# A two-layer gated encoder on one core: ACT, VectorE and GpSimd ordered by a list scheduler inside the kernel, and a feed-forward input projection with 512 weight columns moving

## The chip, the cores and the metric

One core of a Trainium2 chip runs one program. The metric is the device time of one execution in microseconds; where several executions are given, their median counts.

## What is computed

The reference is a bidirectional encoder trunk of two layers on 256 tokens of width 1024, all in float32. In the reference's words, cut to what matters (`B` is 1, `S` 256, `D` 1024, the hidden width `FFN_HIDDEN` 2816):

```python
for l in range(DEPTH):                       # 2 layers
    h = rms_norm(x, norm_mix_pre[l])
    (c_q, c_kv, k_rope, sc_b, sc_c, sc_x, cf_a, cf_g, gm_u, gm_v, gate_logits) = split(h @ w_in[l])
    y_a = mla_branch(c_q, c_kv, k_rope, ...) @ w_o_mla[l]       # 8-head attention
    y_b = short_conv_branch(sc_b, sc_c, sc_x, ...) @ w_o_sc[l]  # 3 taps
    y_c = conformer_branch(cf_a, cf_g, ...) @ w_o_cf[l]         # 31 taps, layer norm, silu
    y_d = gmlp_branch(gelu(gm_u), gelu(gm_v), ...) @ w_o_gm[l]  # spatial gating
    g = sigmoid(gate_logits + gate_b[l])
    merged = g[0] * y_a + g[1] * y_b + g[2] * y_c + g[3] * y_d
    x = x + rms_norm(merged @ w_out[l], norm_mix_post[l])
    f_g, f_u = split(rms_norm(x, norm_ffn_pre[l]) @ w_ffn_in[l])
    x = x + rms_norm((silu(f_g) * f_u) @ w_ffn_out[l], norm_ffn_post[l])
```

## The kernel before, in words

**Numbers.** TensorE reads its operands in a reduced format (fp32r), so every weight and every activation is split into a high part (a cast on ACT) and a low part (raw minus high, on VectorE), and each product is three matmuls: high by high, high by low, low by high (lines 207 to 209 in `group`; 458 to 460 and 880 to 882 are the same three written out). Attention's two products (lines 677 and 703), the spatial gating (570) and all transposes against an identity (214) are plain float32.

**Weights.** They arrive in units of about 1 MB, 2048 columns of 128 partitions (`unit_list`, class `Weights`). A unit is loaded into one of 4 raw buffers by a DMA of the SP queue (line 138), cast to `hi` on ACT (line 173, in two pieces of 1024) and subtracted to `lo` on VectorE (line 176), into one of 5 pairs of buffers; `use` hands a pair out, `free` gives it back and starts the next. The SP queue is in order: a load that waits for a raw buffer holds those behind it, the rows of gains and biases (`brow`, `gain`) too.

**TensorE.** There are two ways of a projection. In `b_unit` the weights stand still (128 columns) and all 256 tokens move: one matmul writes 128x256, and the result comes out transposed, with the features on the partitions. In the other a tile of 128 tokens (`hth`, `htl`) stands still and 512 weight columns move: one matmul writes 128x512, and what a later product needs transposed goes through TensorE's transposes. The feed-forward input uses the second way for the first 512 hidden units (line 850 on) and `b_unit` for the other 2304: nine blocks of 256 units, each a gate and an up matrix (lines 853 to 858 follow them: silu, product, split).

**Order.** TensorE's and SP's instructions run in the order of the program. Side work on TensorE (attention, the conformer's transposes, the spatial gating, the turns of a tile) is written as generators; `start` puts one in a heap with a due time, and `tick` after each group of three matmuls resumes those that are due by a clock of counted matmul times, with fixed waits (STEP 9, ROPE 14, GMS 12, PACE 2 and so on). The four AV matmuls of a head pair (`values`, line 703) are yielded singly. ACT, VectorE and GpSimd are put in order by the tile framework, by program order; the conformer's 120 tap operations per layer (line 526, VectorE) are held back by a priority of 100, and are issued two at a time. PSUM has 4 banks `pb` for projections and 4 `psd` for side work.

**Places that the steps touch.** `gt` (line 789) adds the gate's bias and frees a bank; `cn` (408) is the normed query and key compression and frees two; `xn` (539) is the conformer's normed row and is what the transposes after it read.

Of the kernel before, what the change touches and what calls it, by code (L numbers as in the profile page):

```python
# [44 lines left out]
def unit_list():  # L45
# [34 lines left out]
    for j in range(2, FH // 256):  # L80
        for o in (0, FH):
            add("w_ffn_in", 0, D, slice(o + 256 * j, o + 256 * (j + 1)))
# [12 lines left out]
def hybrid_encoder(ctx: ExitStack, tc: tile.TileContext, wts, x_in, pos, invf, cols, rows, wst, out):  # L95
    nc = tc.nc
    act, dve, pool, pe = nc.scalar, nc.vector, nc.gpsimd, nc.tensor
# [6 lines left out]
    LAG = 1.0  # L104
    LATE, PACE = 100, 2.0
    WARM = 34
    P1 = 3.0
    TRS = 7.0
    GMS = 12.0
    STEP = 9.0  # L110
    APART = 1.5
    ROPE = 14.0
    NORM = 8.0
    MTURN = 2.5
# [16 lines left out]
    def bank(s="pb"):  # L131
        return ps.tile([P, 512], F32, tag="pb", name=nm(s), bufs=4)

    def sbank(s="psd"):
        return ps.tile([P, 512], F32, tag="psd", name=nm(s), bufs=4)

    def load(dst, src):
        tc.keep_in_program_order(nc.sync.dma_start(dst, src))
# [8 lines left out]
    class Weights:  # L147
        def __init__(self):
            self.nd = self.ns = self.n = self.nf = 0
            self.splits = {}  # L150
            self.raw, self.parts = {}, {}

        def load(self, i):
            l, u = divmod(i, NU)
            w = widths[u]
# [4 lines left out]
            for c in range(0, w, step):  # L160
                load(t[:, c : c + step], src[:, c : c + step])
            self.raw[i] = t

        def split(self, i):
# [13 lines left out]
        def fill(self, apart=0.0):  # L178
            while self.ns < min(self.nf + B_HI, L * NU):
                while self.nd < min(self.ns + B_RAW, L * NU):  # L180
                    self.load(self.nd)
                    self.nd += 1
                self.splits[self.ns] = start(self.split(self.ns), apart * self.ns)
                self.ns += 1

        def use(self, n):
            i = self.n
            self.n += 1
            drain(self.splits.pop(i))
            w = widths[i % NU]  # L190
            return tuple(a[:, :w].rearrange("p (k n) -> p k n", n=n) for a in self.parts.pop(i))
# [7 lines left out]
    def split(hi, lo, src):  # L199
        act.copy(hi, src)  # L200
        dve.tensor_tensor(lo, src, hi, op=ALU.subtract)  # L201

    def group(o, terms, first=True, last=True):
        n = len(terms)
        cost = 3 * o.shape[-1] / 2370.0 if len(o.shape) == 2 else 3 * S / 2370.0
        for i, (lh, ll, rh, rl) in enumerate(terms):
# [3 lines left out]
            tick(cost)  # L210

    def transposes(o, ins, rows_out=P):
        for j, a in enumerate(ins):
            pe.transpose(out=o[:rows_out, j * P : (j + 1) * P], in_=a, identity=ident)  # L214
            clock[0] += 0.11
# [7 lines left out]
    def rstd_of(r, ms, eps=EPS):  # L223
        pool.tensor_scalar(r, ms, eps, None, op0=ALU.add)
        pool.tensor_tensor(r, r, mhalf[:, : ms.shape[-1]], op=ALU.pow)
# [37 lines left out]

    def rope_tables():
        pi = small(T, "pi")
        pii = sb.tile([P, T], I32, tag="pii", name="pii")
        for t in range(T):
            load(pii[:, t : t + 1], pos[0, t * P : (t + 1) * P].rearrange("(p o) -> p o", o=1))
        dve.tensor_copy(pi, pii)
        fr = small(16, "fr")  # L270
        load(fr, invf)
# [23 lines left out]
    def pre_norm(t, g):  # L295
# [3 lines left out]
        act.activation(h, x[:, t, :], AF.Square, scale=D ** -0.5, accum_out=ss)  # L299
        rstd_of(r, ss)  # L300
        for j in range(2):
            c = slice(512 * j, 512 * (j + 1))
            dve.scalar_tensor_tensor(h[:, c], x[:, t, c], r, g[:, c], op0=ALU.mult, op1=ALU.mult)

        def turn():
            for j in range(2):
                b = sbank()
                transposes(b, [h[:, 512 * j + P * k : 512 * j + P * (k + 1)] for k in range(4)])
                bv = b.rearrange("p (k n) -> p k n", n=P)
                split(hth[:, t, 4 * j : 4 * j + 4, :], htl[:, t, 4 * j : 4 * j + 4, :], bv)  # L310
            yield None
# [3 lines left out]
    def post_norm(t, banks, g, store=False):  # L315
# [4 lines left out]
        for j in range(2):  # L320
            c = slice(512 * j, 512 * (j + 1))
            sq = slot(s="sq")
            act.activation(sq, banks[j], AF.Square, scale=D ** -0.5, accum_out=ss[:, j : j + 1])
            if j == 0:
                pool.tensor_scalar(s1, ss[:, 0:1], EPS, None, op0=ALU.add)
            dve.tensor_tensor(y[:, c], banks[j], g[:, c], op=ALU.mult)
        rstd_of(r, ss[:, 1:2], s1)
        for j in range(2):
            c = slice(512 * j, 512 * (j + 1))
            dve.scalar_tensor_tensor(x[:, t, c], y[:, c], r, x[:, t, c], op0=ALU.mult, op1=ALU.add)  # L330
            if store:
                nc.sync.dma_start(out[t * P : (t + 1) * P, c], x[:, t, c])
# [16 lines left out]
    @contextmanager  # L349
    def later(n):  # L350
        at = tc.cur_priority
        tc.cur_priority = at + n
        yield
        tc.cur_priority = at

    clock = [0.0]
    waiting = []

    def start(g, after=0.0):
        heapq.heappush(waiting, (clock[0] + after, nm("g"), g))  # L360
        return g

    def tick(us):
        clock[0] += us
        while waiting and waiting[0][0] <= clock[0]:
            due, _, g = heapq.heappop(waiting)
            after = next(g, None)
            if after is not None:
                heapq.heappush(waiting, (max(due + after, clock[0] + min(after, 0.3)), nm("g"), g))

    def drain(g):
        for i, w in enumerate(waiting):
            if w[2] is g:
                waiting.pop(i)
# [596 lines left out]
```

## Time and profile before

| | |
|---|---|
| median of 3 runs | 972.03 us (971.9 to 972.37) |
| the profiled execution, its own time | 973.39 us |
| its span, first to last instruction | 971.6 us |
| TensorE (PE) busy | 955.2 us, 98% of the span |
| weight loads of TensorE (PEld) | 860.4 us, 89% |
| VectorE (DVE) | 672.5 us, 69% |
| ACT | 477.2 us, 49% |
| GpSimd (POOL) | 46.1 us, 5% |
| read from HBM | 177.63 MB, 184 GB/s over the span |

Matmuls are pipelined and their ends are modelled, so the busy time of PE overlaps itself: what a matmul costs is read from the start of one to the start of the next. A wait in brackets behind a row is idle time of the engine before it, with what ended it. A float32 matmul leaves two records (two passes), a transpose and a matmul of split parts one. DVE is VectorE.

### The profile page before, as it was taken

What the parts mean: (1) busy time and instruction counts of PE and PEld (TensorE: products, weight loads), DVE (VectorE), ACT (ScalarE), POOL (GpSimd) and SP (SyncE); (2) the same over time, 40 slices, a digit from 0 to 9 for tenths busy, and PEclk for the clock granted to TensorE, in tenths of its full rate; (3) what the DMA queues carried; (4) which work ended last, traced back from release to release, by engine and by line L of the source; (5) the groups of instructions that cost most, each with busy time, mean ns of one, the idle gap of its engine ahead of it and who ended that gap; (6) DMA issues with size and microseconds to landing.
All of it is one profiled execution on the core that took longest, in us unless ns stands there. A gap on an engine that the chain in (4) does not pass through costs nothing.

```text
span 971.6 us, 14463 instructions
## 1 busy us (share of the span) xinstructions
PE 955.2 (98%) x5890; PEld 860.4 (89%) x5890; DVE 672.5 (69%) x998; ACT 477.2 (49%) x712; POOL 46.1 (5%) x87
## 2 busy tenths in 40 slices
PE   8999999999999999999999999999999999999997
PEld 7999987888888999998889999888888889999885
DVE  5789999676757655554377899986767675555432
ACT  6555654564445644443365655545544554444421
POOL 1100000010002000000110000000000110000000
PEclk9999999999999999999999999999999999999999
DMA  8765455435654655564268554554365366555601
GB/s 345 274 239 196 152 183 175 162 130 217 206 184 174 217 174 180 193 234 167 100 228 292 174 174 162 173 178 159 141 237 185 122 213 233 191 174 174 224 15 44
DMA packets 29731, 179.62 MB, mean 185 GB/s; under 512 B 3680, under 2 KB 3808, under 8 KB 10208
## 3 DMA queue, kind: packets, MB, share of 16 engines
q1 hardware_dynamic: 29664, 178.69, 52.3%
q8 instruction: 46, 0.75, 0.3%
q14 instruction: 21, 0.17, 0.1%
HBM read 177.63 MB, written 1.05 MB: 184 GB/s over the span
## 4 chain that ended last, share of the span: by engine, by line
PE 86%; DVE 10%; DMA 1%; issue 1%; POOL 1%; ACT 0%; SPq 0%; DVEq 0%; POOLq 0%
PE pb L207 22%; PE pb L209 22%; PE pb L208 22%; PE acc L881 4%; PE acc L880 4%; PE acc L882 4%; DVE yc L526 4%; DVE lo L176 4%; PE psd L214 2%; PE psd L677 1%; PE pb L460 1%; PE pb L459 1%; PE pb L458 1%; PE av L703 1%; DMA brow<-in_rows_dram 1%
## 5 line engine op out<-in xcount | busy, mean ns | idle before, releaser
L176 DVE TENSOR_TENSOR lo<-raw,hi 128x1024 fp32r<-128x1024 f32 (+4 forms) x321 | 379.0, 1200 | 143.2 <-ACT hi L173 143.2
L173 ACT CAST hi<-raw 128x1024 fp32r<-128x1024 f32 (+4 forms) x321 | 323.6, 1035 | 304.5 <-issue 191.1
L207 PE MATMUL pb<-hth,hi 128*128 128x256 f32 x960 | 274.3, 286 | 0.0
L209 PE MATMUL pb<-hth,lo 128*128 128x256 f32 x960 | 271.7, 283 | 0.0
L208 PE MATMUL pb<-htl,hi 128*128 128x256 f32 x960 | 271.6, 283 | 0.0
L208 PEld LDWEIGHTS pb<-htl,hi 128*128 128x128 f32 x960 | 184.0, 192 | 0.3
L207 PEld LDWEIGHTS pb<-hth,hi 128*128 128x128 f32 x960 | 184.0, 192 | 0.3
L209 PEld LDWEIGHTS pb<-hth,lo 128*128 128x128 f32 x960 | 183.9, 192 | 0.0
L207 PE MATMUL pb<-hi,hth 128*128 128x512 f32 x352 | 143.8, 409 | 2.4 <-DVE gt L789 2.4
L209 PE MATMUL pb<-hi,htl 128*128 128x512 f32 x352 | 137.5, 391 | 0.0
L208 PE MATMUL pb<-lo,hth 128*128 128x512 f32 x352 | 137.3, 390 | 0.0
L526 DVE SCALAR_TENSOR_TENSOR yc<-zc,hcol,yc 128x241 f32<-128x241 f32 (+14 forms) x240 | 97.7, 465 | 0.0
L209 PEld LDWEIGHTS pb<-hi,htl 128*128 128x128 f32 x352 | 66.1, 188 | 14.5 <-DVE htl L201 0.3
L207 PEld LDWEIGHTS pb<-hi,hth 128*128 128x128 f32 x352 | 66.3, 188 | 13.9 <-DVE gt L789 2.7
L208 PEld LDWEIGHTS pb<-lo,hth 128*128 128x128 f32 x352 | 66.4, 189 | 11.5
L880 PE MATMUL acc<-hi,fh 128*128 128x512 f32 x176 | 68.6, 390 | 0.0
L881 PE MATMUL acc<-lo,fh 128*128 128x512 f32 x176 | 68.5, 389 | 0.0
L882 PE MATMUL acc<-hi,fl 128*128 128x512 f32 x176 | 68.5, 389 | 0.0
L880 PEld LDWEIGHTS acc<-hi,fh 128*128 128x128 f32 x176 | 33.0, 188 | 6.8
L881 PEld LDWEIGHTS acc<-lo,fh 128*128 128x128 f32 x176 | 33.1, 188 | 6.8
L882 PEld LDWEIGHTS acc<-hi,fl 128*128 128x128 f32 x176 | 33.0, 188 | 6.8
L858 DVE TENSOR_TENSOR f<-f,pb 128x512 f32<-128x512 f32 x18 | 12.4, 687 | 37.7 <-PE pb L209 37.7
(185 smaller groups left out, 1107.0 us busy)
## 6 DMA issues: line engine op xcount, KB each, us to landing
raw<-in_wts_dram SPq DMA_DIRECT2D x152, 1024.0 KB, 4.8
brow<-in_rows_dram SPq DMA_DIRECT2D x24, 256.0 KB, 5.0
gain<-in_rows_dram SPq DMA_DIRECT2D x8, 512.0 KB, 5.7
raw<-in_wts_dram SPq DMA_DIRECT2D x3, 816.0 KB, 4.2
raw<-in_wts_dram SPq DMA_DIRECT2D x2, 768.0 KB, 7.6
raw<-in_wts_dram SPq DMA_DIRECT2D x2, 544.0 KB, 6.2
x<-in_x_dram SPq DMA_DIRECT2D x2, 512.0 KB, 6.0
out_dram<-x SPq DMA_DIRECT2D x4, 256.0 KB, 2.0
```

Source lines behind the costliest of these rows:

```text
L173: act.copy(h[:, c:e], raw[:, c:e])
L176: dve.tensor_tensor(lo[:, c:e], raw[:, c:e], h[:, c:e], op=ALU.subtract)
L207: pe.matmul(o, lh, rh, start=(first and i == 0), stop=False)
L208: pe.matmul(o, lh, rl, start=False, stop=False)
L209: pe.matmul(o, ll, rh, start=False, stop=(last and i == n - 1))
L214: pe.transpose(out=o[:rows_out, j * P : (j + 1) * P], in_=a, identity=ident)
L458: pe.matmul(o, lh, wh[:, k % 3, c], start=(k == 0), stop=False)
L526: dve.scalar_tensor_tensor(y[:, f, a:e], ft2(zc[j])[:, f, a + k - CPAD : e + k - CPAD], cw[:, ff, k : k + 1], y[:, f, a:e], op0=ALU.mult, ...
L858: dve.tensor_tensor(f, f, b, op=ALU.mult)
L880: pe.matmul(o, lh, w[0][:, k, c], start=st, stop=False)
L881: pe.matmul(o, lh, w[1][:, k, c], start=False, stop=False)
L882: pe.matmul(o, ll, w[0][:, k, c], start=False, stop=sp)
```

## The change

**The scheduler.** Calls on ACT, VectorE, GpSimd and on SP's stores no longer emit instructions. They go into a list with a modelled cost and a rank. `Tensor.step` advances a clock by a modelled time for each matmul and then lets `pump` issue, engine by engine, the operation that can start first by the model, and the one of lowest rank among those ready within 0.01 us. Ranks: -0.5 for the norms, 0 for the split of a weight unit that is next to be used, 1 for the rest, 2 for the conformer's taps, 3 for splits further ahead. The order so found is the program's: all five engines then run in order. Loads are issued when the split that frees their buffer is issued in the model. In SP's queue the first row of gains of the second layer (`brow`, read by `cn`) so stands behind six weight loads of that layer, before behind eight; on ACT the order holds nine table loads in place of eight.

**TensorE's side work.** A generator now yields what it needs (`need`), and `poll` resumes it when the model says that this is written and a bank is free; the fixed waits are gone except STEP (9 to 7). `values` yields after two AV matmuls with nothing to wait for, so all four of a head pair follow each other.

**The feed-forward input.** All hidden units are done with tokens standing and 512 weight columns moving (the last block has 256 gate and 256 up columns); each result is transposed on TensorE and split from PSUM (`f_turn`).

The core of the diff:

```diff
+    def cost_act(op, outs, ins):
+        return width(outs[0]) / 1200.0 + 0.195 + 0.05 * (len(ins) > 1) + 0.19 * (len(outs) > 1)
+    def cost_dve(op, outs, ins):
...
+        return n / 960.0 + 0.16 + 0.05 * (op == "scalar_tensor_tensor")
+    def cost_pool(op, outs, ins):
+        return 0.57 if op == "tensor_tensor" else 0.28
...
+    def issue(o):
...
+        at[e] = t = max(at[e], o.ready()) + o.cost
+        for r in o.outs:
+            mark(done, r, t + 0.08)
...
+        o.emit()
+    def event(until):
...
+            t = min(f[0] for f in free)
+            if t <= until and (best is None or t < best[0]):
+                best = t, min((o for f, o in free if f <= t + 0.01), key=Op.order)
...
+        issue(best[1])
...
+    class Tensor:
+        def step(self, out, ins, us):
+            regs, to = [region(v) for v in ins], region(out)
+            flush(clashes([to], regs))
+            t = max([clock[0], opened.get(out.name, 0.0)] + [when(done, r) for r in regs])
+            clock[0] = t + us
...
+            pump(clock[0])
...
+            def rank():
+                return 0 if i <= self.n + NEAR else 3
             for c, e in spans:
-                act.copy(h[:, c:e], raw[:, c:e])
-            for c, e in spans:
-                yield LAG
-                dve.tensor_tensor(lo[:, c:e], raw[:, c:e], h[:, c:e], op=ALU.subtract)
+                act.copy(h[:, c:e], raw[:, c:e], rank=rank)
+                dve.tensor_tensor(lo[:, c:e], raw[:, c:e], h[:, c:e], op=ALU.subtract, rank=rank, then=self.more if e == w else None)
...
-                        with later(LATE):
-                            dve.scalar_tensor_tensor(y[:, f, a:e], ...)
-                        n += 1
-                        if n % 2 == 0:
-                            yield PACE
+                        dve.scalar_tensor_tensor(y[:, f, a:e], ..., rank=2)
...
             for t in range(T):
-                yield 2.0
+                yield need(*yc)
...
                 for j in range(2):
                     h = 2 * hp + j
                     for kc in range(T):
                         i = 2 * j + kc
                         pe.matmul(av[:, DN * h : DN * (h + 1)], ...)
-                        clock[0] += 0.06
-                        yield 0.3
+                    yield need()
...
-        for j in range(2, FH // 256):
-            b = b_unit()
+        for j in range(1, FH // 512):
+            bs = [bank() for _ in range(T)]
+            both(bs)
+            f = [slot(s="f") for _ in range(T)]
+            for t in range(T):
+                act.activation(f[t], bs[t], AF.Silu)
+            bs = [bank() for _ in range(T)]
+            both(bs)
+            hs, ls = hidden(2)
+            for t in range(T):
+                dve.tensor_tensor(f[t], f[t], bs[t], op=ALU.mult)
+                fts.append(start(f_turn(t, f[t], hs, ls)))
```

**VectorE, first gate of the first layer's short-convolution branch.** Before (`gt` are the two gates, `yc` the conformer's taps, `lo` the splits of weights, `m` the merged sum):

```order
L789 TENSOR_TENSOR gt_1667<-pb_1568,brow_1566 128x512
L176 TENSOR_TENSOR lo_1678<-raw_1459,hi_1677 128x1024 x2
L526 SCALAR_TENSOR_TENSOR yc_507<-zc_505,hcol,yc_507 128x250
L526 SCALAR_TENSOR_TENSOR yc_506<-zc_504,hcol,yc_506 128x249 x2
L526 SCALAR_TENSOR_TENSOR yc_507<-zc_505,hcol,yc_507 128x249 x2
L526 SCALAR_TENSOR_TENSOR yc_506<-zc_504,hcol,yc_506 128x248 x2
L176 TENSOR_TENSOR lo_1723<-raw_1544,hi_1722 128x1024 x2
L789 TENSOR_TENSOR gt_1670<-pb_1569,brow_1566 128x512
```

Now (`o` is an attention output, `rs` its sums):

```order
L175 TENSOR_TENSOR lo_1461<-raw_1394,hi_1460 128x1024 x2
L175 RECIPROCAL rs_1699<-sums_1293 128x8
L175 TENSOR_TENSOR gt_1703<-pb_1591,brow_1589 128x512
L175 TENSOR_TENSOR o_1700<-av_1469,rs_1699 128x512
L175 TENSOR_TENSOR gt_1704<-pb_1592,brow_1589 128x512
L175 SCALAR_TENSOR_TENSOR m_1577<-gt_1703,pb_1705 128x512
L175 SCALAR_TENSOR_TENSOR yc_481<-zc_479,hcol,yc_481 128x253
```

Between the two gates there stood two pairs of splits and seven taps; now there is one attention output.

**TensorE, the AV matmuls of one head pair.** Before:

```order
L703 MATMUL av_1622<-v_924,pt_1522 128x64
L207 MATMUL pb_1568<-hi_1279,hth 128x512
L208 MATMUL pb_1568<-lo_1280,hth 128x512
L209 MATMUL pb_1568<-hi_1279,htl 128x512
L703 MATMUL av_1622<-v_953,pt_1522 128x64
L207 MATMUL pb_1569<-hi_1279,hth 128x512
```

Now, in a short-convolution projection:

```order
L248 MATMUL av_1469<-v_949,pt_1389 128x64
L248 MATMUL av_1469<-v_977,pt_1389 128x64
L248 MATMUL av_1469<-v_949,pt_1389 128x64
L248 MATMUL av_1469<-v_977,pt_1389 128x64
L252 MATMUL psd_1475<-ident,p_1398 128x128 x4
L248 MATMUL psd_1482<-kT_1245,qT_1268 128x256 x2
```

Each AV matmul stood alone between groups of three; now four follow each other, 16 times in the program.

**TensorE, feed-forward input of the first layer after its first 512 hidden units.** Before:

```order
L207 MATMUL pb_3135<-hth,hi_2978 128x256
L208 MATMUL pb_3135<-htl,hi_2978 128x256
L209 MATMUL pb_3135<-hth,lo_2979 128x256
L207 MATMUL pb_3135<-hth,hi_2978 128x256
L208 MATMUL pb_3135<-htl,hi_2978 128x256
```

Now, one block of 512 hidden units later, with the transposes of the block before (`f`, two tiles of tokens):

```order
L248 MATMUL pb_3283<-hi_3129,hth 128x512
L248 MATMUL pb_3283<-lo_3130,hth 128x512
L248 MATMUL pb_3283<-hi_3129,htl 128x512
L252 MATMUL psd_3295<-ident,f_3209 128x128 x4
L252 MATMUL psd_3301<-ident,f_3210 128x128 x4
L248 MATMUL pb_3283<-hi_3129,hth 128x512
```

Over the program 1728 matmuls of 256 columns become 864 of 512, and the transposes of `f` go from 16 to 88.

## Rows read from the trace of the kernel before

**Rows 1.** The page: busy time of each engine; the chain that ended last.
```profile
PE 955.2 (98%) x5890; PEld 860.4 (89%) x5890; DVE 672.5 (69%) x998; ACT 477.2 (49%) x712; POOL 46.1 (5%) x87
...
PE 86%; DVE 10%; DMA 1%; issue 1%; POOL 1%; ACT 0%; SPq 0%; DVEq 0%; POOLq 0%
```

**Rows 2.** Stretches: PE, PEld, DVE, ACT, POOL busy (x count), PE clock, DMA share, GB/s.
```profile
97.20:145.70 48.50, 48.50 (x330) 44.90 (x329) 48.17 (x92) 29.83 (x48) 2.73 (x3) 1.00 0.47 167
340.10:388.60 48.50, 48.50 (x406) 48.50 (x406) 25.03 (x25) 20.11 (x25) 0.00 (x0) 1.00 0.51 177
```

**Rows 3.** Waits of PE: total us, times, longest us.
```profile
PE pb L207 <- DVE gt L789: 2.4, 2, 1.4
PE psd L214 <- DVE xn L539: 1.7, 2, 0.9
PE pb L459 <- DVE lo L176: 1.4, 1, 1.4
...
PE pb L458 <- DVE cn L408: 1.2, 1, 1.2
```

**Rows 4.** Timeline of PE, feed-forward input, 256 columns (start us, us, instruction).
```profile
344.83 0.28 PE L207 MATMUL pb<-hth,hi 128*128 128x256 f32 x1
...
346.75 0.28 PE L208 MATMUL pb<-htl,hi 128*128 128x256 f32 x1
```

**Rows 5.** The same, 512 columns: the first 512 hidden units of the feed-forward input.
```profile
318.02 0.39 PE L208 MATMUL pb<-lo,hth 128*128 128x512 f32 x1
...
321.66 0.39 PE L209 MATMUL pb<-hi,htl 128*128 128x512 f32 x1
```

**Rows 6.** Timeline of PE: eight transposes between matmuls of 512 columns.
```profile
486.31 0.39 PE L882 MATMUL acc<-hi,fl 128*128 128x512 f32 x1
486.55 1.03 PE L214 MATMUL psd<-ident,h 128*128 128x128 f32 x8
...
487.65 0.40 PE L881 MATMUL acc<-lo,fh 128*128 128x512 f32 x1
```

**Rows 7.** Timeline of PE: single AV matmuls (two records each) in a gate, then a wait.
```profile
144.09 0.33 PE L703 MATMUL av<-v,pt 128*128 128x64 f32 x2
144.23 0.48 PE L207 MATMUL pb<-hi,hth 128*128 128x512 f32 x1
...
145.01 0.33 PE L703 MATMUL av<-v,pt 128*128 128x64 f32 x2
...
146.84 0.33 PE L703 MATMUL av<-v,pt 128*128 128x64 f32 x2
148.59 0.50 PE L207 MATMUL pb<-hi,hth 128*128 128x512 f32 x1 [1.42 <-DVE gt L789]
```

**Rows 8.** Timeline of the weight loads behind the first of those AV matmuls.
```profile
144.20 0.19 PEld L207 LDWEIGHTS pb<-hi,hth 128*128 128x128 f32 x1
144.31 0.19 PEld L208 LDWEIGHTS pb<-lo,hth 128*128 128x128 f32 x1
```

**Rows 9.** Timeline of DVE ahead of the wait that ends at 148.59.
```profile
140.00 0.69 DVE L789 TENSOR_TENSOR gt<-pb,brow 128x512 f32<-128x512 f32 x1
...
142.86 2.80 DVE L526 SCALAR_TENSOR_TENSOR yc<-zc,hcol,yc 128x250 f32<-128x250 f32 x7
145.58 2.35 DVE L176 TENSOR_TENSOR lo<-raw,hi 128x1024 fp32r<-128x1024 f32 x2
147.85 0.68 DVE L789 TENSOR_TENSOR gt<-pb,brow 128x512 f32<-128x512 f32 x1
```

**Rows 10.** Timeline of DVE where the second layer begins.
```profile
502.94 0.88 DVE L408 SCALAR_TENSOR_TENSOR cn<-pb,c,brow 128x256 f32<-128x256 f32 x2 [2.14 <-DMA brow<-in_rows_dram]
```

**Rows 11.** Groups by line and shape, GpSimd and ACT (xcount, busy us, mean ns, idle).
```profile
L681 POOL TENSOR_SCALAR mx<-mx 128x2 f32<-128x2 f32 x16 | 8.5, 529 | 294.0 <-DVE mx L680 294.0
...
L173 ACT CAST hi<-raw 128x1024 fp32r<-128x1024 f32 x311 | 318.6, 1049 | 302.8 <-issue 191.1 <-PE pb L209 72.7 <-PE acc L882 17.1
...
L684 ACT ACT_TABLE_LOAD x2 | 2.6, 1283 | 0.0
```

More of the change, by code (lines that the diff above doesn't have):

```diff
@@ L96, in hybrid_encoder, with mark, when @@
     nc = tc.nc
-    act, dve, pool, pe = nc.scalar, nc.vector, nc.gpsimd, nc.tensor
+    clock = [0.7]
+    at = {"ACT": 0.7, "DVE": 0.7, "POOL": 0.7, "SP": 0.7}
+    dma = [1.5]
+    done, last, touch = {}, {}, {}
+    def mark(d, r, t):
+        k = d.setdefault(r[0], {})
+        k[r[1:]] = max(k.get(r[1:], 0.0), t)
+    def when(d, r):
+        return max([t for (lo, hi), t in d.get(r[0], {}).items() if lo < r[2] and r[1] < hi], default=0.0)
+    pending = {e: [] for e in at}
+    seq = [0]
@@ new lines, in cost_pool, with ready, order, clashes @@
+    def cost_pool(op, outs, ins):
+        return 0.57 if op == "tensor_tensor" else 0.28
+    class Op:
+        def ready(self):
+            return max([self.since] + [when(done, v) for v in self.ins] + [when(last, v) for v in self.outs])
+        def order(self):
+            return (self.rank() if callable(self.rank) else self.rank), self.n
+    def clashes(outs, ins):
+        found = []
+        for regs, writes in ((outs, True), (ins, False)):
+            for n, lo, hi in regs:
+                for p in touch.get(n, ()):
+                    if any(m == n and a < hi and lo < b for m, a, b in (p.outs + p.ins if writes else p.outs)):
+                        found.append(p)
+        return found
@@ L129, in small, with oldest, psum, bank @@
         return sb.tile([P, n], F32, tag=f"c{n}", name=nm(s), bufs=8 if n < 8 else 4)
[L131 to L138, printed above, removed]
+    rings = {"pb": [], "psd": []}
+    held = set()
+    def oldest(tag):
+        return next(b for b in rings[tag] if b not in held)
+    def psum(tag, s, hold):
+        b = ps.tile([P, 512], F32, tag=tag, name=nm(s), bufs=4)
+        n = b[:, 0:1].name
+        if len(rings[tag]) == 4:
+            old = oldest(tag)
+            rings[tag].remove(old)
+            flush(list(touch.get(old, ())))
+            opened[n] = max(last.get(old, {}).values(), default=0.0) + 0.05
+        rings[tag].append(n)
+        if hold:
+            held.add(n)
+        return b
+    def bank(s="pb", hold=False):
+        return psum("pb", s, hold)
+    def sbank(s="psd", hold=False):
+        return psum("psd", s, hold)
+    def load(dst, src, after=0.0):
+        nc.sync.dma_start(dst, src)
+        n = 4.0 * width(dst) * dst.shape[0]
+        dma[0] = max(dma[0], clock[0] + 1.0, after + 1.0) + n / 400e3
+        mark(done, region(dst), dma[0] + 1.8)
     units = unit_list()
@@ L188, in use @@
             self.n += 1
-            drain(self.splits.pop(i))
+            while i not in self.parts:
+                flush(list(pending["DVE"][:1]))
             w = widths[i % NU]
@@ L477, in layer @@
         if l == 0:
-            with tc.manual_schedule(engines={mybir.EngineType.Activation, mybir.EngineType.DVE}):
-                first()
-                for f, t in steps:
-                    if f is gated and t == 0:
-                        gm_rows()
-                    f(t)
+            first()
+            for f, t in steps:
+                if f is gated and t == 0:
+                    gm_rows()
+                    tables()
+                f(t)
         else:
@@ L869, in layer @@
         TAIL = 4
-        acc = [[(bank if t == 0 else sbank)("acc") for _ in range(2)] for t in range(T)]
+        acc = [[(bank if t == 0 else sbank)("acc", True) for _ in range(2)] for t in range(T)]
         def ffn_out(t, j, w, ns=(0, 1)):
```

353 lines of the change are left out of this document (226 added, 127 removed).

## The prediction

> **What bounds the kernel now.** I read the page first, then the stretches, then the waits of TensorE, then single timelines. On the page [rows 1] the reader is to see TensorE busy for 98% of the span and holding 86% of the chain that ended last; no other engine passes 69%. So a microsecond counts only if TensorE spends it. The stretches [rows 2] show two kinds of work: in the feed-forward input (340 to 389 us) TensorE is full, VectorE and ACT are at 25.03 and 20.11 of 48.50 us; in the mixing part (97 to 146 us) TensorE and VectorE are full together, VectorE at 48.17 of 48.50. [...] TensorE's own waits [rows 3] are few: two for the gate addition, 2.4 us; two for the conformer's row, 1.7; one for a low part at the start, 1.4; one for the query compression at the second layer's start, 1.2. That is 6.7 us in six places. The change can thus win in two ways alone: cheaper TensorE work, or these six waits.
>
> **Part 1, 512 columns moving.** A matmul of 256 columns follows the last one after 1.92 us / 16 = 0.120 us (first and last of 17 starts) [rows 4]. One of 512 columns, in the very form that the change uses, follows after 3.64 / 16 = 0.2275 us (17 starts again) [rows 5]. Each pair that becomes one saves 2 x 0.120 - 0.2275 = 0.0125 us. 1728 matmuls become 864: 864 x 0.0125 = **10.8 us saved**.
> [...]
>
> **Part 2, the new transposes.** 72 more of 128x128. From the matmul at 486.31 to that at 487.65 lie 1.34 us, of which two matmuls of 512 take 0.455 and eight transposes the other 0.885: 0.111 each [rows 6]. 72 x 0.111 = **8.0 us added**, all on TensorE. Their results are split out of PSUM in pieces of 256; half of ACT and VectorE is idle there [rows 2], and each block's transposes have the 10.9 us of the next block's gate (48 x 0.2275) to be split in, so I cost that at nothing. Should that cover fail, PSUM banks would come free late, and the pieces themselves, some 5 us per layer on either engine, would be the most it could cost. Parts 1 and 2 together: -2.8 us.
>
> **Part 3, AV matmuls in fours.** A lone one costs (145.01 - 144.09) - 3 x 0.2275 = 0.24 us [rows 7]. Each has two records with a weight load each. The trace has no two AV matmuls in a row, so I bound. Near end: the load behind the AV records starts 0.11 us before the next [rows 8]; if that is the pace of loads, eight records take 0.88, plus the 0.02 that a lone one has beyond its two loads, 0.90 against 4 x 0.2375 = 0.95. 16 groups x 0.05 = 0.8 us. Far end: the matmul behind a lone AV starts 0.14 us after it [rows 7]; at 0.14 for each of the three that no longer end in a switch, a group saves 3 x 0.0975 = 0.29, and 16 groups 4.7 us. The bound below is nothing. I take **0.8 us saved**, since the row of loads is about what 64 columns cannot hide.
>
> **Part 4, the six waits.** The wait that ends at 148.59 takes 148.59 - 146.84 = 1.75 us where a lone AV is followed after 0.14: 1.61 lost for an idle time of 1.42 [rows 7], so each wait costs 0.19 more than it shows, and six cost 6.7 + 6 x 0.19 = 7.8 us. The two for the gate: the second gate addition came 7.85 us after the first, behind splits and seven taps of 2.80 us [rows 9]. In the new order one attention output stands between them; both waits go. The two for the conformer's row: its transposes were put by a fixed wait of 2.0 us; now they are resumed only when the row is written, so they go. The one for the query compression: VectorE stood 2.14 us for a row of gains [rows 10], whose load SP held behind eight weight loads of that layer; now it stands behind six, and the wait should go with it. The one at the start: the second tile's norm and its two low parts went ahead of the weight's low part; now the weight is ahead, and the transposes come when the tile is ready. I keep 1.5 us there, for the loads are dense at the start and something else is late next. **6.3 us saved**, between 0 and 7.8.
>
> **Part 5, what the frozen order adds.** All engines now run in the order of a model. It takes 0.28 us for a GpSimd addition that the trace shows at 529 ns, and knows no table loads of 1283 ns [rows 11]; there are now 9 of these, before 8. TensorE's side work is resumed as soon as the model calls its input written, so what is 0.25 us late can hold TensorE: 16 softmax steps x 0.25 = 4.0 us at most from that, and nothing at least, since the model takes 0.47 us for a tap that the trace does in 0.40 [rows 9], and so runs behind the chip on VectorE. I take **1.5 us added**, nearer the low end, because most groups of taps are longer than one softmax step's error. Splits of weights, loads, casts and the tail after the last matmul keep their number and place; SP's and GpSimd's queues issue the same instructions.
>
> **The sum.** -10.8 + 8.0 - 0.8 - 6.3 + 1.5 = -8.4 us. Against the profiled execution, 973.4 us (its span 971.6 and 1.8 around it), that is 965.0. That execution was 1.4 us above the median of 972.0, so I forecast **963.6 us**, 0.9% faster. Its own range is 960 to 968: the waits' and the frozen order's bounds partly used.
>
> **The rivals.**
> *AV at the far end.* Part 3 gives 4.7 instead of 0.8: 959.7 us. For it: AV's two records start close together. Against: no two loads in these rows follow each other faster than 0.11. [...]
> *Waits swapped, not removed.* The six go, and as many microseconds come back where side work or a bank is late in the model's order: only parts 1 to 3 remain, -3.6, so 968.4 us. For it: 4.0 us of softmax error, table loads unmodelled. This also covers a scheduler whose order is no better than the framework's.
> *Slower: splits just in time.* While taps are left, a weight unit is split ahead of them only once it is next to be used. From there TensorE has one unit, 24 x 0.2275 = 5.5 us. Two casts of 1.05 us [rows 11] and a last low part of 1.2 (half of 2.35) [rows 9] need 3.3 at least. The margin is 2.2 us. A table load (1.28), a tap under way (0.40) and a late GpSimd step (0.25) at once take 1.9 of it; an operation that waits for TensorE, such as the attention output between the two gates, can take the rest. Beyond the margin, TensorE stands for each unit. Some 32 units (16 per layer) are split like this; 0.5 us each is 16 us: 979.6. It makes the kernel slower from 8.4 / 32 = 0.26 us a unit on. For it: VectorE has no slack in that stretch [rows 2]. Against: the urgent split is ahead of the taps by rank, and the taps are shorter than modelled.
> *The merging saves nothing.* If the 512 form cost 0.240 in the long blocks, 10.8 us would be missing: 974.4. [...] Against it stands the same form at 0.2275 in the same projection [rows 5].
>
> **How the numbers follow.** Forecast 0.60, AV far end 0.14, waits swapped 0.13, splits just in time 0.10, merging for nothing 0.03. A measurement of this kernel tells about 0.2%, or 1.9 us, from no change. Faster, below 970.1: nearly all of the first two and two thirds of the third, 0.80 with a little taken off for what I have not seen. Slower, above 974.0: the last two at 0.12. The same: 0.08. The range of 957 to 972 takes in the AV rival but for its low end and the swapped waits; outside lie some 0.05 below and 0.12 above.
>
> **What would show it.** In the profile after: the pitch of the feed-forward input at 0.2275 us throughout, with bursts of eight transposes worth 0.9 us; AV groups of four at about 0.90 us; no wait of TensorE for the gate, the conformer's row or the query compression, and small ones, below 0.3 us, ahead of transposes of the softmax. TensorE waits on low parts (`lo`), repeated unit by unit between 90 and 260 us, would prove the forecast wrong by the slower rival; a sum of waits above 6 us would prove part 4 wrong.

## The result and the profile after

The changed kernel takes 981.99 us (median of 4 runs, 981.91 to 982.16) against 972.10 for the kernel before (median of 4): a ratio of 1.0102, 95% interval 1.0084 to 1.0119, so 1% slower. The forecast was 963.6, range 957 to 972. The profiled execution took 981.91 us, its span is 980.1, and the granted clock is 0.999 (before 0.996).

First the page of the changed kernel: busy time of the engines, and the chain that ended last (they answer to [rows 1]).

```profile
PE 966.4 (99%) x5098; PEld 818.5 (84%) x5098; DVE 670.3 (68%) x1018; ACT 476.2 (49%) x733; POOL 44.5 (5%) x87
...
PE 94%; DVE 2%; ACT 1%; issue 1%; DMA 1%; POOL 1%; SPq 0%; DVEq 0%; POOLq 0%; ACTq 0%
```

TensorE has 792 matmuls fewer and is busy 11 us longer; its share of the chain grew from 86% to 94%. So it waits less and works longer. The stretches that answer to [rows 2], with the same columns (the mixing part; the feed-forward input):

```profile
100.00:148.50 48.50, 48.50 (x330) 44.59 (x329) 38.94 (x68) 27.98 (x53) 1.74 (x5) 1.00 0.41 147
342.00:390.50 48.50, 48.50 (x219) 39.20 (x218) 24.30 (x28) 21.31 (x30) 0.00 (x0) 1.00 0.52 183
```

VectorE is no longer full in the mixing part (38.94 of 48.50 us, before 48.17), and TensorE is full in both. The waits of TensorE (total us, times, longest), against [rows 3]:

```profile
PE pb L248 <- DVE lo L175: 3.3, 3, 1.5
PE warm L252 <- POOL mhalf L175: 1.3, 1, 1.3
PE pb L248 <- ACT hth L175: 1.0, 1, 1.0
PE pb L248 <- DVE htl L175: 0.4, 2, 0.2
PE psd L252 <- DVE h L175: 0.4, 1, 0.4
```

The waits for `gt`, `xn` and `cn` are gone, as forecast. The prediction's 6.7 us left out four more waits of the kernel before:

```profile
PE warm L903 <- POOL ident masks.py:199: 1.4, 1, 1.4
...
PE pb L458 <- ACT hth L200: 1.1, 1, 1.1
PE psd L214 <- DVE h L303: 0.5, 1, 0.5
PE pb L460 <- DVE htl L201: 0.4, 1, 0.4
```

All listed waits come to 10.1 us before and 6.4 after, so waits can't explain 10 us more. What a matmul costs can. TensorE's timeline after, in the 256-column form (a block of the mixing part) and in the 512-column form of the feed-forward input, each with the first and last of 17 starts, against [rows 4, 5]:

```profile
63.04 0.28 PE L248 MATMUL pb<-hth,hi 128*128 128x256 f32 x1
...
64.93 0.28 PE L248 MATMUL pb<-htl,hi 128*128 128x256 f32 x1
...
345.35 0.39 PE L248 MATMUL pb<-hi,htl 128*128 128x512 f32 x1
...
349.08 0.39 PE L248 MATMUL pb<-hi,hth 128*128 128x512 f32 x1
...
437.44 0.40 PE L248 MATMUL acc<-hi,fl 128*128 128x512 f32 x1
...
441.18 0.40 PE L248 MATMUL acc<-hi,fh 128*128 128x512 f32 x1
```

256 columns: 1.89 / 16 = 0.118 us, before 0.120. 512 columns: 3.73 / 16 = 0.2331, before 0.2275. The last two rows are the feed-forward output, whose matmuls the change does not touch; 17 starts lie 3.74 us apart, 0.2337 each. The same product in the kernel before:

```profile
437.35 0.39 PE L882 MATMUL acc<-hi,fl 128*128 128x512 f32 x1
...
440.98 0.39 PE L880 MATMUL acc<-hi,fh 128*128 128x512 f32 x1
```

3.63 / 16 = 0.2269. The 512-column matmuls became some 6 ns dearer whatever stands still: the means are 233.2 ns with `hth` and `htl`, 233.3 with `fh` and `fl` and 233.3 with the others, before 227.6, 226.8 and 227.5. There are 3072 of them now. That is where the time is. No step of the prediction and no rival had it.

### The profile page after: what moved, and what is told of

It reads as the page before. It is cut to its first block, busy times and chain, and to the rows that moved or that the text cites. A ratio compares the mean times of both kernels' runs of the same rounds, so it can differ in the third digit from the quotient of the medians.

```text
span 980.1 us, 12950 instructions
## 1 busy us (share of the span) xinstructions
PE 966.4 (99%) x5098; PEld 818.5 (84%) x5098; DVE 670.3 (68%) x1018; ACT 476.2 (49%) x733; POOL 44.5 (5%) x87
## 4 chain that ended last, share of the span: by engine, by line
PE 94%; DVE 2%; ACT 1%; issue 1%; DMA 1%; POOL 1%; SPq 0%; DVEq 0%; POOLq 0%; ACTq 0%
PE pb L248 74%; PE acc L248 13%; PE psd L252 4%; PE psd L248 2%; PE av L248 1%; DVE lo L175 1%; DMA raw<-in_wts_dram 1%; POOL c L175 1%; ACT hi L175 1%; DVE h L175 0%; ACT h L175 0%; DVE x L175 0%; SPq L308 0%; DVE htl L175 0%; ACT sq L175 0%
## 5 line engine op out<-in xcount | busy, mean ns | idle before, releaser
L248 PE MATMUL pb<-hi,hth 128*128 128x512 f32 (+1 forms) x704 | 275.7, 392 | 1.0 <-ACT hth L175 1.0
L248 PE MATMUL pb<-lo,hth 128*128 128x512 f32 (+1 forms) x704 | 271.5, 386 | 3.3 <-DVE lo L175 3.3
L248 PE MATMUL pb<-hi,htl 128*128 128x512 f32 (+1 forms) x704 | 271.6, 386 | 0.6 <-DVE htl L175 0.4
L248 PEld LDWEIGHTS pb<-hi,htl 128*128 128x128 f32 x704 | 132.0, 187 | 31.0 <-DVE htl L175 2.0
L248 PE MATMUL pb<-hth,hi 128*128 128x256 f32 x384 | 109.2, 284 | 0.0
L248 PE MATMUL pb<-hth,lo 128*128 128x256 f32 x384 | 107.9, 281 | 0.0
L248 PE MATMUL pb<-htl,hi 128*128 128x256 f32 x384 | 107.9, 281 | 0.0
L248 PEld LDWEIGHTS pb<-htl,hi 128*128 128x128 f32 x384 | 72.4, 189 | 0.3
L248 PEld LDWEIGHTS pb<-hth,hi 128*128 128x128 f32 x384 | 72.4, 188 | 0.3
L248 PEld LDWEIGHTS pb<-hth,lo 128*128 128x128 f32 x384 | 72.4, 188 | 0.0
```

The source lines that it names most:

```text
L248: nc.tensor.matmul(out, lhsT, rhs, **k)
```

## The experiments

One piece of the change stands in no step of the prediction, nor in the cut of its diff above. The position and frequency tiles of the rope tables are now allocated at setup:

```diff
+    pii = sb.tile([P, T], I32, tag="pii", name="pii")
+    fr = small(16, "fr")
+
+    def tables():
```

Tiles get addresses in the order in which their pools are first asked for them. `pii` takes 32 bytes of a partition and the four buffers of `fr` 256, and so `hi` and `lo`, allocated behind them, moved by 288 bytes (addresses in a partition, as in the built programs): `hi` from 144704 to 144992, `lo` from 185664 to 185952. The stationary tiles `hth`, `htl` (27712 on) and the slots (85056 on) stayed. Two theories were set against each other: A, the place of `hi` and `lo` sets the pitch; B, the new order of the other engines does, by their traffic or semaphores.

**e1, the small tile wider.**

```diff
-    pii = sb.tile([P, T], I32, tag="pii", name="pii")
+    pii = sb.tile([P, 16], I32, tag="pii", name="pii")[:, :T]
```

> The changed kernel with one number altered: the integer position tile is 16 columns wide instead of 2 (64 bytes per partition instead of 8, which took 32), so that every tile allocated behind it, the weight tiles hi and lo first, stands 32 bytes further: hi at 145024, a multiple of 64, where the changed kernel has 144992 and the kernel before 144704. The order of every engine stays. Theory A (the place of hi and lo sets the pitch of a matmul that streams 512 columns from them): the pitch falls from 0.2335 to 0.227 us, 3072 x 0.0067 = 20.6 us less, 961.4 us, within 1.5. Theory B (the new order of the other engines slows the streaming, by traffic or by semaphores): pitch 0.2335, 982 us as the change had.

Measured: 967.83 us, ratio to before 0.995 (0.9938 to 0.9963). 32 bytes gave 14 us back, with the instructions of every engine in the same order, so B falls. My 961.4 was too low: the pitch is 0.229 on average and not 0.227, and 256 columns take 0.1165: a multiple of 64 is not the whole rule.

**e2, the kernel before with the two tiles allocated early.** The two lines move from `rope_tables` to setup, nothing else.

> The kernel before with the two tiles of the rope tables allocated at setup, as the change does, and nothing else: hi moves from 144704 to 144992. Theory A: its 2208 matmuls of 512 columns go to 0.2335 us, 14.8 us more; if the fall of the 256-column pitch from 0.120 to 0.118 comes from the same cause, 2880 x 0.0017 = 4.9 of it comes back: between 982 and 987 us. Theory B: 972 us, pitches as before.

Measured: 979.39 us, ratio 1.0069 (1.0055 to 1.0083). The old kernel becomes slow by the allocation alone: mean pitch of 512 columns 227.4 to 233.2 ns, of 256 columns 120.6 to 119.0 (starts over 290 ns apart left out). 17 starts of its feed-forward output:

```profile
442.16 0.39 PE L883 MATMUL acc<-hi,fl 128*128 128x512 f32 x1
...
445.89 0.39 PE L881 MATMUL acc<-hi,fh 128*128 128x512 f32 x1
```

3.73 / 16 = 0.2331, where the kernel before has 0.2269. Over the pairs that follow each other directly, the two traces differ by 11.64 us for 512 columns and -4.55 for 256, 7.1 together; measured were 6.8. My 982 to 987 was too high: it had 6.7 ns for every matmul of 512 columns.

**e3, `lo` alone off its place.** The small tile is allocated between `hi` and `lo`.

```diff
             h = sb.tile([P, UW], F32R, tag="hi", name=nm("hi"), bufs=B_HI)
+            if i == 0:
+                tab.append(sb.tile([P, T], I32, tag="pii", name="pii"))
```

> The changed kernel with hi at 144704 as in the kernel before and the small tile allocated between hi and lo, so that lo alone stands 32 bytes off a multiple of 64. Theory A: the third of the 512-column matmuls that stream lo take 0.2335 us, the two thirds that stream hi 0.227: 961.4 + 1024 x 0.0067 = 968.3 us. A form of A in which the distance between hi and lo matters: all three alike, at 0.227 or at 0.2335. Theory B: 982 us, all at 0.2335.

Measured: 976.61 us, ratio 1.0041 (1.0025 to 1.0056); a miss in size. From a matmul that streams `hi` to the next that streams `hi` it is 226.8 ns, from `hi` to `lo` 231.0, from `lo` to `hi` 236.1. So `hi` at its old place is fast, as A says, but one tile out of line costs 13 ns in three matmuls where I had 6.7. The step from `lo` to `hi` takes more than either place alone (227 and 233); the mean of the three, 231.3, lies between them.

**e4, the feed-forward projection alone, in the kernel before.** Its core:

```diff
-        for j in range(2, FH // 256):
-            b = b_unit()
...
+        for j in range(1, FH // 512):
+            bs = [bank() for _ in range(T)]
+            both(bs)
...
+                fts.append(start(f_turn(t, f[t], hs, ls), 2.5))
```

> The kernel before with the feed-forward projection of the change alone (512 weight columns moving, 72 transposes more), the other engines ordered as before, hi at 144704. By parts 1 and 2 of the prediction, with the pitches of the kernel before: -10.8 + 8.0 = -2.8, 969.2 us, 512-column pitch 0.227 throughout. Theory B with the merged form itself as the cause: pitch 0.2335 in all of it, 972 + 8 + 2208 x 0.0067 = 990 us or more.

Measured: 969.02 us against 972.59, ratio 0.9963 (0.995 to 0.9975); mean pitch of 512 columns 227.3 ns. 3.6 us saved, 2.8 forecast. In the traces, input and output of the feed-forward part together are 1.6 us shorter in each layer than before (186.19 against 187.82 in the first), 3.2 in all. With the tiles where [rows 4, 5] had them, parts 1 and 2 hold.

**e5, the tiles back, all else of the change kept.** The two tiles are allocated inside `tables`, behind `hi` and `lo`; the order of all five engines is the changed kernel's.

> The changed kernel with the two small tiles allocated where their loads are issued, behind the weight tiles, so that hi and lo stand at the addresses of the kernel before (144704 and 185664); the order of the engines stays. If the place of hi and lo explains the whole difference of pitch, 512 columns take 0.227 us again: from the run with the wide tile (967.8, pitch 0.229 to 0.232), about 3072 x 0.0038 = 11.7 us less for the 512 columns and 1152 x 0.002 = 2.3 more for the 256: 958 to 964 us, and the rest of the prediction (sum -8.4) can be read from it. If the wide tile's 967.8 is already all that the place gives, 968.

Measured: 966.52 us against 972.71, ratio 0.9935 (0.9921 to 0.9948). The place alone is worth 981.99 - 966.52 = 15.5 us. The sum over the pitches agrees: from start to start, the 3011 pairs of 512-column matmuls take 711.0 us in the changed kernel and 693.7 here, the 1140 pairs of 256 columns 136.2 and 138.0: -17.3 + 1.8 = -15.5. My 958 to 964 was too low: against e1, 512 columns gain 1.9 ns where I had 3.8, and 256 columns lose 3.6 where I had 2.0, so 967.8 - 5.9 + 4.1 = 966.0.

**e6, everything 32 bytes further.** As e5, and a tile ahead of all others is longer.

```diff
-    warm = cp.tile([P, 2], F32, name="warm")
+    warm = cp.tile([P, 16], F32, name="warm")[:, :2]
```

> As the run before it, but a tile at the very start is 32 bytes longer, so that everything behind it, the moving hi and lo and the stationary slots and hth alike, stands 32 bytes further (hi 144736, hth 27744, slots from 85088; all no multiple of 64 now). Theory A1 (a start that is no multiple of 64 is read slower): pitch 0.2335, 20 us more than the run before it. Theory A2 (what counts is where the moving tile stands against the stationary one, whose load goes on beside it): pitch 0.227 and the same time as the run before it, within 2 us.

Measured: 966.48 us, ratio 0.9934 (0.9921 to 0.9948), the same as e5. Its timeline in the feed-forward output, 17 starts again:

```profile
429.25 0.39 PE L248 MATMUL acc<-hi,fl 128*128 128x512 f32 x1
...
432.88 0.39 PE L248 MATMUL acc<-hi,fh 128*128 128x512 f32 x1
```

3.63 / 16 = 0.2269. None of these tiles starts at a multiple of 64 now, and nothing is slower. A1 falls: what counts is where tiles stand against each other.

**e7 and e8, a sweep.** As e5, with buffers of unlike places.

```diff
-            h = sb.tile([P, UW], F32R, tag="hi", name=nm("hi"), bufs=B_HI)
-            lo = sb.tile([P, UW], F32R, tag="lo", name=nm("lo"), bufs=B_HI)
+            h = sb.tile([P, UW + 8], F32R, tag="hi", name=nm("hi"), bufs=B_HI)
+            if i == 0:
+                sb.tile([P, 24], F32, tag="pad1", name="pad1")
+            lo = sb.tile([P, UW + 8], F32R, tag="lo", name=nm("lo"), bufs=B_HI)
```

e8 has one more tile of 128 bytes ahead of them.

> As the run with the tiles late, but hi and lo are 32 bytes longer each, so that their five buffers stand 0, 32, 64, 96 and 128 bytes off the place of the kernel before against the stationary tiles, the same for hi and its lo. Read by buffer: 0 off gives 0.227 us and 32 off 0.2335 (both seen), 64 off 0.229 to 0.230. A1 expects 64 and 128 off at the value of 0 off or near it and 96 off at that of 32; A2 has no number for 96 and 128 and expects an even course. Total between 962 and 975 us.

> The same with the buffers at 128, 160, 192, 224 and 256 bytes off. If 256 off repeats 0 off (0.227), the period is 256 bytes or a part of it; the value at 128 must agree with the run before. A1: 160 and 224 at 0.2335. Whether a place gives under 0.2265 for 512 columns, or under 0.117 for 256, decides what the best placing is.

Measured: 976.69 and 979.40 us (one execution each); the upper end of my total was too low. By buffer, the mean from start to start in ns (starts over 290 ns apart left out; two values where both runs had the place):

```
hi and lo minus hth, modulo 256    0            32     64     96     128          160    192    224
512 columns (hi, lo move)          228.3 228.1  233.2  229.9  233.5  232.6 232.4  234.0  232.8  233.4
256 columns (hi, lo stand still)   120.3 119.8  118.7  115.8  118.4  118.6 119.0  120.3  117.8  116.8
```

256 bytes off repeats 0 off. For 512 columns the kernel before stands on the best of eight places; for 256 columns that same place is one of the two worst. The changed kernel stands at 32. Where a whole kernel stands at one place, its mean agrees with the sweep: 227.2 ns at 0 (e5), 233.3 at 32 (the changed kernel), 229.1 at 64 (e1), 233.2 at 224 (e10, below).

**e9, one number of the model.** With e5's places, 966.5 is still 2.9 us above the forecast. TensorE's waits in e5:

```profile
PE pb L248 <- DVE lo L175: 3.9, 3, 1.5
PE warm L252 <- POOL mhalf L175: 1.3, 1, 1.3
PE pb L248 <- ACT hth L175: 1.2, 1, 1.2
PE pb L248 <- DVE htl L175: 0.4, 2, 0.2
```

Two of the three for `lo` lie where no wait was before: at the start of the feed-forward input, in each layer. Timelines of PE, VectorE and GpSimd there (start us, us):

```profile
307.08 0.39 PE L248 MATMUL pb<-hi,hth 128*128 128x512 f32 x1
308.67 0.50 PE L248 MATMUL pb<-lo,hth 128*128 128x512 f32 x1 [1.20 <-DVE lo L175]
...
301.81 3.49 DVE L175 TENSOR_TENSOR lo<-raw,hi 128x1024 fp32r<-128x1024 f32 x3
306.06 1.41 DVE L175 SCALAR_TENSOR_TENSOR h<-x,c,gain 128x512 f32<-128x512 f32 x2 [0.77 <-POOL c L175]
307.40 2.35 DVE L175 TENSOR_TENSOR lo<-raw,hi 128x1024 fp32r<-128x1024 f32 x2
...
303.24 2.14 POOL L175 TENSOR_SCALAR c<-c 128x1 f32<-128x1 f32 x1 [3.45 <-ACT h L175]
305.46 0.57 POOL L175 TENSOR_TENSOR c<-c,mhalf 128x1 f32<-128x1 f32 x1
```

VectorE stands 0.77 us for the second tile's norm, with the low part that TensorE wants queued behind it: the model took 0.28 us for a GpSimd addition that here lasts 2.14, and so put the norm first.

```diff
-        return 0.57 if op == "tensor_tensor" else 0.28
+        return 0.57 if op == "tensor_tensor" else 0.53
```

> The kernel with the tiles late (966.5 us), with one number of the model altered: a GpSimd addition costs 0.53 us in the model instead of 0.28, as the trace of before had it (529 ns). In the order, both low parts of the third weight unit of the feed-forward input then stand ahead of the second tile's normalisation on VectorE, in both layers; before, one of the two stood behind it. Theory P (TensorE's four waits at the start of the feed-forward input, 3.3 us in two layers, come from this order: VectorE stands 0.77 us for a GpSimd step with the needed low part queued behind it): three of the 3.3 us go, 963.5 us, within 1. Rival Q (these low parts are late anyway, by the loads or the ACT casts): the waits stay, 966 us.

Measured: 964.31 us, ratio 0.991 (0.9895 to 0.9925), 2.2 us less than e5. The waits now:

```profile
PE pb L248 <- ACT hth L175: 1.6, 4, 0.9
PE warm L252 <- POOL mhalf L175: 1.3, 1, 1.3
PE pb L248 <- DVE htl L175: 1.1, 3, 0.7
```

None for `lo` is left, so theory P holds; smaller ones for the second tile's `hth` and `htl` came in, which is why 2.2 and not 3. In the traces e9 gains 1.1 us at each start of the feed-forward input and 0.3 at the start of the program, where the order changed as well and a wait for `lo` of 1.5 us went too. The GpSimd addition still lasts 2.13 us and VectorE still stands 0.77: what changed is which low part stands ahead of the norm.

**e10, the stationary tiles alone.** As e5, with `hth` and `htl` 32 bytes further against everything else.

```diff
+    cp.tile([P, 8], F32, name="pad0")
     hth = cp.tile([P, T, KD, P], F32R, name="hth")
     htl = cp.tile([P, T, KD, P], F32R, name="htl")
+    cp.tile([P, 56], F32, name="pad1")
```

> The kernel with the tiles late, and hth and htl alone 32 bytes further; hi, lo, the slots, raw all keep their places against each other (all 256 bytes further). Theory A2 (moving against stationary tile): the 1920 matmuls of 512 columns with hth or htl as stationary go from 0.228 to about 0.2333 us (place 224 of the sweep), those with fh, mh and the branch operands stay at 0.227, and the 256-column form, whose moving operand is hth, goes from 0.120 to about 0.117: +10.2 - 3.6, some 973 us. Rival A3 (moving tile against what the other engines read and write, raw and the slots): all pitches stay, 966.5 us.

Measured: 973.43 us, ratio 1.0004 (0.9995 to 1.0013), 6.9 above e5. In one execution, the feed-forward input, where `hth` stands still (12 starts), and the output, where `fh` does (17 starts):

```profile
344.63 0.40 PE L248 MATMUL pb<-hi,hth 128*128 128x512 f32 x1
...
347.19 0.39 PE L248 MATMUL pb<-hi,htl 128*128 128x512 f32 x1
...
431.79 0.39 PE L248 MATMUL acc<-hi,fh 128*128 128x512 f32 x1
...
435.42 0.39 PE L248 MATMUL acc<-lo,fh 128*128 128x512 f32 x1
```

2.56 / 11 = 0.2327 against 3.63 / 16 = 0.2269, with the same `hi` and `lo`, raw tiles and slots, and all the engines in the same order. A3 falls. It is the moving tile against the stationary one. The means say the same: 233.2 ns with `hth` or `htl` standing still (227.2 in e5), 226.9 with `fh` or `fl` (226.9).

**e11, each form at its best place.** The weights of the 256-column form are written 64 bytes into buffers that are 256 bytes longer; that takes room, so a slot goes.

```diff
-    B_RAW, B_HI, B_SLOT, B_BIG, B_GAIN = 4, 5, 25, 2, 2
+    B_RAW, B_HI, B_SLOT, B_BIG, B_GAIN = 4, 5, 24, 2, 2
...
+            s = 16 if units[i % NU][2] - units[i % NU][1] == D else 0
+            h = sb.tile([P, UW + 64], F32R, tag="hi", name=nm("hi"), bufs=B_HI)[:, s : s + w]
+            lo = sb.tile([P, UW + 64], F32R, tag="lo", name=nm("lo"), bufs=B_HI)[:, s : s + w]
```

> The kernel with the model's 0.53, one slot fewer (24), hi and lo buffers 256 bytes longer each (at 0 off against the stationary tiles), and the weights that stand still in the 256-column form written 64 bytes into their buffer, where the sweep gave 115.8 ns instead of 119.9. The 512-column form stays at 0.227. 1152 x 0.0041 = 4.7 us less than the run with the model's 0.53: 958.8 us if that is at 963.5. If the slot that is missing makes work late, 960 to 965.

Measured: 966.31 us, ratio 0.9931 (0.9918 to 0.9943), 2.0 more than e9. The pitches came nearly as forecast (227.1 and 116.4 ns) and gave 1152 x 3.6 ns = 4.1 us, but a new wait took as much, some 2.1 us in each layer with the return, and a stretch behind the first of the two took the rest:

```profile
PE psd L252 <- ACT p L175: 3.5, 2, 1.8
```

```profile
160.50:163.40 2.90, 2.90 (x8) 2.26 (x7) 2.90 (x4) 1.41 (x2) 0.00 (x0) 0.51 0.00 0
```

```profile
161.40 0.63 PE L248 MATMUL pb<-hi,hth 128*128 128x512 f32 x1
161.83 0.63 PE L248 MATMUL pb<-lo,hth 128*128 128x512 f32 x1
```

TensorE had stood idle for 1.75 us until 158.44. Then the granted clock was 0.51 (ahead of the last two figures of the row), and matmuls of 512 columns lay 0.43 us apart in place of 0.227: 1.7 us lost in this execution. Behind the second wait, as long, the clock stayed at 1.00. The five executions of e11 lie between 964.93 and 967.82 us, wider than those of any other run here.

**e12, the same with all slots, `hi` alone shifted.** Only `hi` gets the longer buffer, so 25 slots fit.

> The kernel with the model's 0.53 and all 25 slots, the five hi buffers 256 bytes longer each, and hi (not lo) written 64 bytes into its buffer for the 256-column form. If the waits of the last run (3.5 us for the softmax, twice at the same step) came from the missing slot, they are gone. If each matmul's pitch follows the place of its own stationary tile, two thirds of the 1152 matmuls save 4.1 ns, 3.1 us: 961.2 us against 964.3. If the load of a lo at another place next to a hi costs, as the run with lo alone off its place showed for 512 columns, nothing is won: 964 us.

Measured: 961.89 us against 972.26, ratio 0.9894 (0.9878 to 0.9911): the fastest version here, ahead of both kernels. Its waits of TensorE, and from its timeline the first and last of 17 starts of the 256-column form:

```profile
PE pb L248 <- ACT hth L175: 1.9, 4, 1.2
PE warm L252 <- POOL mhalf L175: 1.3, 1, 1.3
PE pb L248 <- DVE htl L175: 1.1, 3, 0.7
```

```profile
62.01 0.28 PE L248 MATMUL pb<-hth,hi 128*128 128x256 f32 x1
...
63.90 0.28 PE L248 MATMUL pb<-htl,hi 128*128 128x256 f32 x1
```

The wait for `p` is gone with the slot back. Apart from the place of `lo` the slot is the only difference, and the order of all engines in e11 was e9's, so the missing slot had most likely made the wait. 1.89 / 16 = 0.118 us: all three matmuls gain about 2 ns (means 118.2, 118.2, 117.4), and not two of them 4. The forecast of 961.2 was near, its division between the three was not.

## Why the prediction was wrong, step by step

**Part 1** is the step that failed, and in it the sentence that takes the pitch "in the very form that the change uses" from [rows 5]. A row gives the price of a form with its tiles where they stand; I took it for the price of the form. At the changed kernel's mean of 233.3 ns the merging saves 864 x (2 x 120 - 233.3) = 5.8 us and not 10.8. And the sum had no term for the matmuls that the change leaves alone: 2208 of 512 columns cost 2208 x 5.9 ns = 13.0 us more (means 227.4 and 233.3), 1152 of 256 columns 1152 x 1.6 = 1.8 less. 5.0 + 13.0 - 1.8 = 16.2 us; the measured 15.5 is less by the waits at the feed-forward input (below), 2.6 us in the changed kernel and 3.3 in e5, where TensorE is faster. That the two tiles were moved stood in the change, and I gave it no line.

**Part 2**, 8.0 us for 72 transposes, stands together with part 1 in e4: -3.6 measured, -2.8 forecast. The cover held: e4's list of waits has none for a bank or for a split of the transposed results. The pieces put there at some 5 us per layer, with no row named, last 0.37 us on ACT and 0.42 on VectorE in the kernel before: 18 more in a layer are 6.7 and 7.6 us.

**Part 3**, 0.90 us for four AV matmuls. After, eight records and the next float32 matmul behind them:

```profile
117.88 1.00 PE L248 MATMUL av<-v,pt 128*128 128x64 f32 x8
118.71 0.61 PE L252 MATMUL psd<-ident,p 128*128 128x128 f32 x4
```

0.83 us, before the return to split matmuls: 0.055 from the first record to the second and 0.11 for each one behind. Eight of the 16 groups are followed by a split matmul itself: it starts 0.81 us after the group's first record, and the next one 0.08 us later than the pitch, 0.89 in all. The near end was right, and the rival of the far end falls.

**Part 4.** The six waits went, but for the 1.5 us that I kept at the start, and that is what the longest wait for `lo` in e5 takes. That nothing would come in their place was wrong: the four waits at the feed-forward input (two in each layer: 1.36 + 0.27 and 1.37 + 0.28 over the pitch in e5) cost 3.3 us. The listed waits of e5 come to 6.8 us, above the 6 that the prediction named as the sign against this part, and 3.3 below the 10.1 of before, not 6.3. Nor was the wait for `cn` sure to be there: with the row of gains behind eight weight loads as before, it stands neither in e2's list nor in e4's. The traced execution of before was 1.4 us above its median, so that wait may not have been in the median that I took its 1.4 us from; no run shows it.

**Part 5.** The mechanism was named, a GpSimd step that the model takes at 0.28 us; its size and its place were off. I priced it at 0.25 us a step in the softmax, at most 4.0 in all. The 529 ns behind that are of no addition: the row in [rows 11] is the softmax's scaling of two columns, and the same 16 steps take 360 ns on average in e5. The softmax shows no wait, and the one step that mattered lasted 2.14 us, in the norm ahead of the feed-forward input. Parts 3 to 5 together were forecast at -5.6; e5 against e4, each beside its own runs of before, gives -6.2 + 3.6 = -2.6. Each ratio is known to some 1.3 us. The missing 3.0 is close to those four waits: in the two traces the feed-forward input, from its first matmul to the first of the output, takes 127.1 us in e5 and 125.2 in e4, in either layer, 3.7 more in all, and the rest of the program some 6 less, near the 5.6 forecast. e9 has 2.2 of it back.

**The rivals.** No wait for a low part repeats unit by unit between 90 and 260 us: the time went above the slower rival's 979.6 without its mechanism. "The merging saves nothing" named the right direction and the wrong cause; by it the 512 form would have been dear in the long blocks alone, and the feed-forward output shows it everywhere. The swapped waits took part of what was won, with 3.3 of 6.3 us.

So 963.6 became 981.99 by 15.5 us of place (e5 against the changed kernel), and by 3.0 us of parts 4 and 5, less 0.8 of parts 1 and 2; the other 0.7 is the kernel before itself, at 972.7 beside e5.

## What to carry to other kernels

When an edit allocates a tile earlier, later or in another size, write down where the operands of the dominant matmuls stand before and after, and whether their distance modulo 256 bytes (in e7 and e8, 512 columns took 228.3 ns at 0 and 228.1 at 256 bytes, and 229.9 to 234.0 at the seven places between) changed; where it did, the old rows may no longer give the price. If a pitch rises by the same few per cent in instructions that the edit never touched, look at addresses before orders and waits: e1 and e2 need a line or two each. An order that is frozen by a model should be read at the places where an urgent operation stands behind one that waits for another engine, with the longest duration that the trace has for that engine, not the usual one.

## What the chip showed that was not expected

**Pitch by place.** 512 fp32r columns take from 227.2 ns with the moving tile at 0 bytes modulo 256 from the stationary one (e5) to 234.0 at 160 (e8), and moving everything by 32 bytes together changes nothing (e6: 966.48 us against 966.52 in e5). No step of the prediction lets the place of the two against each other count; here 32 bytes on the stationary side alone cost 6.0 ns of 227 (e10). Whether it is the load of the next weights that meets the stream, or something else in the pair, no run here tells apart.

**Even the best place is not the columns alone.** 227.1 ns for 512 columns (e11) and 120 for 256 (0 in the sweep) differ by 107 for 256 columns, so some 13 ns of each lie beside the columns (estimated from these two). But 256 columns stand at one of their dearer places there (120.3 and 119.8 ns, against 115.8 at 64). With the 116.4 of e11 the same estimate gives 111 for 256 columns and leaves some 6 ns.

**GpSimd behind VectorE.** The addition on one column lasted 2.14 us from 303.24, to 305.38; VectorE's three low parts ended at 301.81 + 3.49 = 305.30, so 0.08 us earlier. In the second layer of e5, 0.09 us earlier:

```profile
776.15 2.14 POOL L175 TENSOR_SCALAR c<-c 128x1 f32<-128x1 f32 x1 [3.45 <-ACT h L175]
...
774.71 3.49 DVE L175 TENSOR_TENSOR lo<-raw,hi 128x1024 fp32r<-128x1024 f32 x3
```

The same addition takes 0.22 us where VectorE stands idle (the first row below, e5; in the changed kernel at 293.72) and also beside a VectorE operation that reads PSUM (`h<-pb,gain`; in the changed kernel at 300.95). Here it lasted over two low parts in a row and ended behind them. That is not always so; a like step of two columns came through within such a row, which lasted to 507.76:

```profile
291.20 0.22 POOL L175 TENSOR_SCALAR c<-c 128x1 f32<-128x1 f32 x1 [2.72 <-ACT h L175]
...
506.33 0.37 POOL L175 TENSOR_SCALAR c<-c 128x2 f32<-128x2 f32 x1 [2.22 <-ACT kr L175]
...
505.40 2.36 DVE L175 TENSOR_TENSOR lo<-raw,hi 128x1024 fp32r<-128x1024 f32 x2
```

What decides between the two, and what holds the addition, no run here shows.
